# A two-layer diffusion backbone on one core: weight parts by casting and accumulating transfers, a three-step normalisation, attention outputs joined and laid out by DMA

## The chip, the cores and the metric

The kernel runs on one core of a Trainium2 chip. The metric is the device time of one execution in microseconds, read from the median of several runs. The core's engines are TensorE (PE; its weight loads are listed as PEld), VectorE (DVE), ScalarE (ACT), GpSimd (POOL) and SyncE (SP), which only issues transfers. SBUF is the memory on the core, PSUM the one into which TensorE writes, and DRAM the chip's own.

## The reference

The input is 512 latent tokens x and 256 context tokens of 1024 channels, and a conditioning vector. Two layers follow each other. The context tokens share the weights; in the second layer they are only needed for keys, values and scan states.

```
for l in range(DEPTH):                                    # 2
    z  = modulate(rms_norm(x, g1), shift, scale) @ w_in    # A: 1024, B: 2048, q, k, v, gates: 3*1024
    ya = rglru_bidir(z_A)      # short convolution, gates r and i by blocks of 64 channels,
                               # a = exp(-8 r softplus(-lam)), u = t i sqrt(1 - a^2), scan in both directions
    yb = spatial_gating(gelu(z_B))
    yc = windowed_attention(q, k, v, k_ctx, v_ctx, sink)   # 16 heads of 64, 4 key/value heads
    x  = x + ga1 * ((sigmoid(gate_a)*(ya@wa) + sigmoid(gate_b)*(yb@wb) + sigmoid(gate_c)*(yc@wc)) @ w_out)
    x  = x + ga2 * (relu(modulate(rms_norm(x, g2), ...) @ w1)**2 @ w2)
```

All of it is in 32-bit floating point.

## The kernel before, in words

**Products in three parts.** Each operand of a large product is split into a rounded part hi (type fp32r) and a remainder lo = src - hi, and the product is hi*hi + hi*lo + lo*hi, three matrix instructions. Activations are split by `split` (line 558): ScalarE copies into hi, VectorE subtracts. Weights come in blocks of 128x1024 (512 KB) through `weights` (line 562): SP's queue loads the tile wr, ScalarE rounds it into wh, and wl = wr - wh is computed by GpSimd where the flag `aside` is set, by VectorE elsewhere. There are three buffers each of wr, wh and wl, and 340 blocks in all.

**Stages of a layer.** First come keys, values and queries, and windowed attention (`attention`, line 1102): four groups of four heads, and in each group one unit for each 128 tokens (six units in layer 0, which carries the context too, four in layer 1). A unit is a softmax (`soft_part`) and the products with the values (`value_part`, line 1071). Between units stand pieces of the next group's queries and, from a list of 24 gate products (`gate_early`), some as filling: 16 in layer 0, 12 in layer 1. Then comes the recurrence (`lru`, line 1140), for eight blocks of 128 channels: a weight block and a block of gate weights (`lru_gates`, line 1131), convolution, gates, and a chain of elementwise instructions with two scans; the rest of the gate products stands between them. Then the merges of the three branches with the spatial gating between them, the output projection (`out_proj`, line 1350), a normalisation (`norm`, line 826), and the feed-forward (`ff`, line 1378). At the end of layer 0 `ff` runs the last part in two streams of tokens, normalises each for the next layer and computes its keys and values.

`aside` is set in the attention, in the part of the output projection that runs by streams, in the first part of the feed-forward, and in the step from layer 0 to layer 1.

**Attention outputs.** After the value products of a unit PSUM holds 128x512: the upper 64 partitions hold a correction that is added to the lower ones, with four heads side by side. Four copies on ScalarE and four additions on VectorE, each 64x128, place the four heads into two tiles of 128 channels. After the last unit of a group both tiles are stored to DRAM (`yd`) from ScalarE's queue; the merge of this branch reads them back through GpSimd's queue.

**Normalisation.** For each of eight channel tiles: VectorE multiplies x with the row factor, which stands in PSUM; ScalarE applies gain and shift; ScalarE copies into hi; VectorE subtracts for lo.

**Order.** All instructions are recorded with their tiles, and a planner (`Rec`, line 182 onward) orders them before they are emitted. Each has an assumed duration (`cost`) and a priority, by its place in the program and a boost for weight loads. The planner plays the engines forward: whichever engine is free takes the ready instruction of best priority, as long as buffers are free. Each engine then runs its instructions strictly in that order. The planner lengthens a VectorE instruction that reads two SBUF operands while GpSimd computes, and takes the size of a transfer from the tile.

Of the kernel before, what the change touches and what calls it, by code (L numbers as in the profile page):

```python
# [18 lines left out]
F32 = mybir.dt.float32  # L19
# [4 lines left out]
OP = mybir.AluOpType  # L24
# [157 lines left out]
class Rec:  # L182
# [91 lines left out]
    def commit(self, calls):  # L274
# [9 lines left out]
        if calls[0][2] == "dma_start":  # L284
            v = (calls[0][6] + calls[0][5])[0]
            op.nbytes = int(np.prod(v.base.shape)) * 4 if not v.base.part else 128 * 768 * 4
# [49 lines left out]
    def schedule(self):  # L336
# [90 lines left out]
        while events:  # L427
# [9 lines left out]
            for e in range(5):  # L437
                while free[e] <= now + 1e-6:
# [21 lines left out]
                    if op.both and free[POOL] > now and busy:  # L460
                        dur += min(0.7 * (free[POOL] - now), dur)
# [66 lines left out]
class Net:  # L528
    def __init__(self, rec, t):
        self.nc = self.rec = rec  # L530
        self.t = t
        self.n = 0
        self.wboost = BOOST
        self.aside = False
# [27 lines left out]
    def weights(self, l, blk):  # L562
        rec = self.rec
# [25 lines left out]
    def setup(self):  # L589
# [14 lines left out]
        self.one = self.ones[:, 0:1]  # L604
        self.neg = self.hold([128, 1], F32, name="neg")
        nc.vector.memset(self.neg, -1.0)
# [464 lines left out]
    def value_part(self, g, b, P, tiles, y2):  # L1071
# [23 lines left out]
        v4 = pv.rearrange("p (f j q) -> p f j q", f=2, j=2)  # L1095
        for f in range(2):
            nc.scalar.activation(y2[f][0:64, qs], v4[64:128, f, 0], AF.Copy)
            nc.vector.tensor_add(y2[f][0:64, qs], v4[0:64, f, 0], y2[f][0:64, qs])
            nc.scalar.activation(y2[f][64:128, qs], v4[0:64, f, 1], AF.Copy)
            nc.vector.tensor_add(y2[f][64:128, qs], v4[64:128, f, 1], y2[f][64:128, qs])  # L1100

    def attention(self, l, hs, W, ps):
# [9 lines left out]
        for g in range(4):  # L1112
            y2 = [self.slot([128, W]) for _ in range(2)]
            for u in range(nu):
                P, tiles = self.soft_part(g, u)
                self.finish(g, u, P, tiles, y2, nu)
# [8 lines left out]
    def finish(self, g, u, P, tiles, y2, nu):  # L1125
        self.value_part(g, u, P, tiles, y2)
        if u == nu - 1:
            for f in range(2):
                self.nc.scalar.dma_start(self.yd[2 * g + f], y2[f])

    def lru_gates(self, l, f):
        nc = self.nc
        gr = self.slot([128, 512])
        nc.sync.dma_start(gr, self.t["gate"][l, f])
        gh = self.slot([128, 512], F32R)
        gl = self.slot([128, 512], F32R)
        self.split(gr, gh, gl)
        return gh, gl

    def lru(self, l, hs, W):  # L1140
# [45 lines left out]
        def recur(pair):  # L1186
            for xc, out in pair:
                for d in range(2):
# [3 lines left out]
                    nc.scalar.activation(r, r, AF.Identity, bias=self.one)  # L1192
# [11 lines left out]
        def chain(xc, out, ss):  # L1204
            for d in range(2):
# [4 lines left out]
                nc.scalar.activation(r, t2, AF.Identity, scale=-0.5, bias=self.neg)  # L1210
# [139 lines left out]
    def out_proj(self, l, W):  # L1350
# [19 lines left out]
        for z in self.streams(W):  # L1370
            self.aside = True
# [6 lines left out]
    def ff(self, l, hs, W):  # L1378
# [33 lines left out]
        self.aside = True  # L1412
# [12 lines left out]
    def run(self):  # L1425
# [6 lines left out]
        for l in range(DEPTH):  # L1432
# [11 lines left out]
            self.aside = True  # L1444
            self.attention(l, hs, W, ps)
            self.aside = False
# [3 lines left out]
            self.aside = False  # L1450
# [124 lines left out]
```

## Time and profile before

| | us |
|---|---|
| median of 3 runs (lowest, highest) | 2715.12 (2712.99, 2715.19) |
| the profiled execution, time | 2712.24 |
| the profiled execution, span from first to last instruction | 2710.5 |
| PE busy | 2624.4 |
| DVE busy | 1868.3 |
| ACT busy | 1239.8 |
| POOL busy | 319.6 |

A busy time is the sum of the stretches in which the engine ran at least one instruction. All recorded instructions carry one line number (L507), that of the helper that emits them; so groups are told apart by tile names: s is any working tile in SBUF, p any in PSUM, t a small one, wr, wh and wl the weight tiles. An arrow s<-p,s reads: written <- read. "Idle before" is the time in which the engine had nothing to run just before the group's instructions, with the instruction that ended it. The chain of waits follows the work that ended last back from the end; PEclk is the clock that TensorE was granted, as a share of full speed.

### The profile page before, as it was taken

To read this page: it belongs to the slowest core of one execution; us is meant where nothing else is said; L and a number is where in the kernel's file an instruction comes from. 1 tells how busy PE (TensorE), PEld (TensorE's weight loads), DVE (VectorE), ACT (ScalarE), POOL (GpSimd) and SP (SyncE) were. 2 spreads that over 40 slices of the span, in tenths; PEclk is the share of its full clock that TensorE was granted. 3 is DMA by queue.
4 is the path that set the end of the run, shared out by engine and by line. 5 is a ranking of instruction groups with operands and counts; after the bars stand their busy time and mean duration, and the time that the engine had idled before them with its cause. 6 is when DMAs were issued, how large, how long until landed. Compare 5 with 4: busy or idle time off the path is not lost.

```text
span 2710.5 us, 38395 instructions
## 1 busy us (share of the span) xinstructions
PE 2624.4 (97%) x14916; PEld 2259.9 (83%) x14916; DVE 1868.3 (69%) x3528; ACT 1239.8 (46%) x2158; POOL 319.6 (12%) x229
## 2 busy tenths in 40 slices
PE   7999999989999999999999998999999999899999
PEld 4889988878898888888888877887888888888887
DVE  8887787996637758544444478999898666844444
ACT  4466668992122225222222254666996223532322
POOL 1111110111000034000000152120011001600000
PEclk9999999989999999999999989999999999999999
DMA  6112122456524423322222232122347555432322
GB/s 241 59 46 69 67 78 83 124 192 201 167 71 161 166 78 111 115 86 86 86 70 63 70 123 70 59 70 95 94 127 252 200 191 174 138 111 93 94 93 86
DMA packets 94391, 309.15 MB, mean 114 GB/s; under 512 B 11328, under 2 KB 11488, under 8 KB 94208
## 3 DMA queue, kind: packets, MB, share of 16 engines
q1 hardware_dynamic: 74592, 248.62, 28.6%
q0 software_dynamic: 10400, 37.09, 4.6%
q10 hardware_dynamic: 9216, 20.98, 2.0%
q8 instruction: 117, 1.92, 0.3%
q14 instruction: 66, 0.54, 0.1%
HBM read 270.99 MB, written 35.65 MB: 113 GB/s over the span
## 4 chain that ended last, share of the span: by engine, by line
PE 73%; DVE 12%; ACT 6%; DMA 4%; issue 4%; POOL 1%; POOLq 0%; SPq 0%; ACTq 0%; DVEq 0%
PE p L507 73%; DVE s L507 8%; ACT s L507 5%; DVE t L507 3%; DMA wr<-wmod 2%; DMA s<-wmod_k 1%; DVE junk L507 1%; POOL wl L507 1%; ACT wh L507 1%; DMA wr<-w 1%; ACT L507 1%; DVE wl L507 1%; DMA s<-x 0%; DMA gn<-qkg 0%; POOLq L1562 0%
## 5 line engine op out<-in xcount | busy, mean ns | idle before, releaser
L507 PE MATMUL p<-s,wh 128*128 128x512 f32 (+1 forms) x6816 | 1673.9, 353 | 6.3 <-DVE s L507 5.9
L507 PEld LDWEIGHTS p<-s,wh 128*128 128x128 f32 x6816 | 1194.7, 189 | 234.9 <-DVE s L507 7.8
L507 PE MATMUL p<-s,wl 128*128 128x512 f32 (+1 forms) x3408 | 1029.8, 352 | 0.3 <-POOL wl L507 0.3
L507 ACT ACTIVATE wh<-wr 128x1024 fp32r<-128x1024 f32 x340 | 360.4, 1061 | 929.6 <-PE p L507 648.1
L507 PEld LDWEIGHTS p<-s,wl 128*128 128x128 f32 x3408 | 572.2, 189 | 48.0 <-POOL wl L507 0.5
L507 DVE TENSOR_TENSOR wl<-wr,wh 128x1024 fp32r<-128x1024 f32 x240 | 294.7, 1228 | 288.3 <-ACT wh L507 285.8
L507 ACT ACTIVATE s<-p 64x128 f32<-64x128 f32 (+6 forms) x718 | 300.4, 452 | 209.8 <-PE p L507 196.1
L507 POOL TENSOR_TENSOR wl<-wr,wh 128x1024 fp32r<-128x1024 f32 x100 | 244.1, 2444 | 1202.7 <-ACT wh L507 1142.6
L507 DVE TENSOR_TENSOR s<-s,s 128x512 fp32r<-128x512 f32 (+5 forms) x409 | 333.8, 834 | 72.1 <-ACT s L507 68.6
L507 PE MATMUL p<-wh,s 128*128 128x256 f32 (+1 forms) x1472 | 303.7, 301 | 4.1 <-DVE s L507 3.5
L507 PE MATMUL p<-s,s 128*128 128x256 f32 (+3 forms) x1568 | 283.9, 322 | 22.5 <-ACT s L507 16.2
L507 ACT ACTIVATE s<-s 128x256 fp32r<-128x256 f32 (+6 forms) x349 | 203.5, 610 | 213.8 <-DVE s L507 201.2
L507 PEld LDWEIGHTS p<-s,s 128*128 128x128 f32 (+1 forms) x1568 | 222.1, 185 | 60.4 <-ACT s L507 21.1
L507 DVE SCALAR_TENSOR_TENSOR s<-p,mod,s 128x512 f32<-128x512 f32 (+1 forms) x222 | 138.1, 645 | 181.4 <-PE p L507 181.4
L507 PEld LDWEIGHTS p<-wh,s 128*128 128x128 f32 x1472 | 238.9, 191 | 16.8 <-DVE s L507 4.4
L507 DVE TENSOR_TENSOR s<-p,s 64x128 f32<-64x128 f32 (+4 forms) x444 | 201.9, 477 | 29.1 <-ACT s L507 23.1
L507 PE MATMUL p<-wl,s 128*128 128x256 f32 (+1 forms) x736 | 219.6, 298 | 0.4 <-DVE wl L507 0.4
L507 DVE SCALAR_TENSOR_TENSOR junk<-wr,condb 128x1024 bf16<-128x1024 f32 x128 | 156.4, 1222 | 73.1 <-DMA wr<-wmod 71.9
L507 PEld LDWEIGHTS p<-wl,s 128*128 128x128 f32 x736 | 140.2, 190 | 6.3 <-DVE wl L507 0.6
L507 ACT ACTIVATE s<-s,t,t 128x512 f32<-128x512 f32 (+1 forms) x128 | 109.8, 861 | 59.4 <-DVE t L507 59.2
L507 PE MATMUL p<-ident,s 128*128 128x128 f32 (+1 forms) x776 | 106.4, 279 | 23.8 <-DVE s L507 21.7
L507 DVE SCALAR_TENSOR_TENSOR s<-s,s 128x768 f32<-128x768 f32 x128 | 116.2, 950 | 12.5 <-ACT s L507 12.5
(87 smaller groups left out, 1322.7 us busy)
## 6 DMA issues: line engine op xcount, KB each, us to landing
wr<-w SPq DMA_DIRECT2D x340, 512.0 KB, 3.6
wr<-wmod SPq DMA_DIRECT2D x80, 512.0 KB, 4.0
gd<-s ACTq DMA_DIRECT2D x24, 384.0 KB, 2.9
s<-gd POOLq DMA_DIRECT2D x24, 384.0 KB, 5.8
s<-x SPq DMA_DIRECT2D x16, 384.0 KB, 6.4
gd<-s ACTq DMA_DIRECT2D x24, 256.0 KB, 2.1
s<-gd POOLq DMA_DIRECT2D x24, 256.0 KB, 5.6
s<-wmod_k SPq DMA_DIRECT2D x16, 256.0 KB, 6.4
```

The lines of the kernel that those rows point to most:

```text
L507: ins = getattr(getattr(self.nc, name), method)(*[r(x) for x in a], **{q: r(x) for q, x in k.items()})
```

## The change

1. In attention and recurrence the flag `cast` is set. `weights` then issues, from GpSimd's queue, a transfer that casts the block from DRAM into wh; ScalarE writes wl = -wh; and a second transfer from GpSimd's queue adds the block from DRAM onto wl. The recurrence's gate blocks are always read so. wr is not used there.
2. `aside` is never set any more, so all other blocks are subtracted on VectorE.
3. `norm`: VectorE multiplies x with gain and row factor in one instruction; ScalarE adds the shift and rounds into hi; VectorE computes (u + shift) - hi.
4. `value_part`: one copy of 64x512 on ScalarE and one addition on VectorE per unit; two stores per unit on SP's queue place the heads in DRAM. The function `finish` and the two group tiles go.
5. Recurrence: two instructions per direction move from ScalarE to VectorE, and the constant tile for them goes.
6. The planner takes the size of a transfer from its view, and lengthens a VectorE instruction by all of GpSimd's remaining time instead of at most 0.7 of it and at most once its own duration.

```diff
@@ commit
-            v = (calls[0][6] + calls[0][5])[0]
-            op.nbytes = int(np.prod(v.base.shape)) * 4 if not v.base.part else 128 * 768 * 4
+            v = [v for v in calls[0][6] + calls[0][5] if not v.base.part]
+            op.nbytes = 512 * v[0].width() if v else 128 * 768 * 4
@@ schedule
-                        dur += min(0.7 * (free[POOL] - now), dur)
+                        dur += free[POOL] - now
@@ weights
-        raw = self.wtile("wr", [128, 1024])
-        rec.sync.dma_start(raw, self.t["w"][l, blk])
+        raw = None if self.cast else self.wtile("wr", [128, 1024])
         hi = self.wtile("wh", [128, 1024], F32R)
         lo = self.wtile("wl", [128, 1024], F32R)
-        self.nc.scalar.activation(hi, raw, AF.Copy)
-        (self.nc.gpsimd if self.aside else self.nc.vector).tensor_sub(lo, raw, hi.bitcast(F32))
+        if self.cast:
+            rec.gpsimd.dma_start(hi, src)
+            rec.scalar.activation(lo, hi.bitcast(F32), AF.Copy, scale=-1.0)
+            rec.gpsimd.dma_start(lo, src, accum_op=OP.add)
+        else:
+            rec.sync.dma_start(raw, src)
+            rec.scalar.activation(hi, raw, AF.Copy)
+            (rec.gpsimd if self.aside else rec.vector).tensor_sub(lo, raw, hi.bitcast(F32))
@@ norm
-            nc.vector.tensor_mul(u, self.x[k][:, a:b], p)
-            nc.scalar.activation(u, u, AF.Identity, scale=G[:, i, k:k + 1], bias=self.mod[l][:, i, sh + k:sh + k + 1])
-            self.split(u, hs[k][0][:, a:b], hs[k][1][:, a:b])
+            shift = self.mod[l][:, i, sh + k:sh + k + 1]
+            h, lo = (t[:, a:b] for t in hs[k])
+            nc.vector.scalar_tensor_tensor(u, self.x[k][:, a:b], G[:, i, k:k + 1], p, op0=OP.mult, op1=OP.mult)
+            nc.scalar.activation(h, u, AF.Identity, bias=shift)
+            nc.vector.scalar_tensor_tensor(lo, u, shift, h.bitcast(F32), op0=OP.add, op1=OP.subtract)
@@ value_part
-        v4 = pv.rearrange("p (f j q) -> p f j q", f=2, j=2)
+        y = self.slot([128, 512])
+        nc.scalar.activation(y[0:64], pv[64:128], AF.Copy)
+        nc.vector.tensor_add(y[0:64], pv[0:64], y[0:64])
         for f in range(2):
-            nc.scalar.activation(y2[f][0:64, qs], v4[64:128, f, 0], AF.Copy)
-            nc.vector.tensor_add(y2[f][0:64, qs], v4[0:64, f, 0], y2[f][0:64, qs])
-            nc.scalar.activation(y2[f][64:128, qs], v4[0:64, f, 1], AF.Copy)
-            nc.vector.tensor_add(y2[f][64:128, qs], v4[64:128, f, 1], y2[f][64:128, qs])
+            d = self.yd[2 * g + f]
+            d = d._with(("rearrange", "(j d) q -> d j q", {"d": 64}), d.ix)
+            d = d._with(("get", (slice(None), slice(None), qs)), d.ix)
+            nc.sync.dma_start(d, y[0:64, f * 256:f * 256 + 256].rearrange("p (j q) -> p j q", j=2))
@@ finish, called after each unit
-        if u == nu - 1:
-            for f in range(2):
-                self.nc.scalar.dma_start(self.yd[2 * g + f], y2[f])
@@ lru_gates
-        nc.sync.dma_start(gr, self.t["gate"][l, f])
-        self.split(gr, gh, gl)
+        nc.gpsimd.dma_start(gh, src)
+        nc.scalar.activation(gl, gh.bitcast(F32), AF.Copy, scale=-1.0)
+        nc.gpsimd.dma_start(gl, src, accum_op=OP.add)
@@ recur and chain
-                    nc.scalar.activation(r, r, AF.Identity, bias=self.one)
+                    nc.vector.tensor_scalar(r, r, 1.0, None, op0=OP.add)
-                nc.scalar.activation(r, t2, AF.Identity, scale=-0.5, bias=self.neg)
+                nc.vector.tensor_scalar(r, t2, -0.5, -1.0, op0=OP.mult, op1=OP.add)
@@ out_proj, and ff before the step into layer 1
-            self.aside = True
@@ run
-            self.aside = True
+            self.aside, self.cast = False, True
             self.attention(l, hs, W, ps)
-            self.aside = False
             self.m = [None] * KT
             conds = (0,) if last else (0, 1)
             ya = self.lru(l, hs, W)
-            self.aside = False
+            self.cast = False
```

## Rows read from the trace of the kernel before

**Rows 1.** The page, part 1: busy us, share of span, instructions.

```profile
PE 2624.4 (97%) x14916; PEld 2259.9 (83%) x14916; DVE 1868.3 (69%) x3528; ACT 1239.8 (46%) x2158; POOL 319.6 (12%) x229
```

**Rows 2.** Stages: length, busy (instructions) of PE, PEld, DVE, ACT, POOL; PEclk, DMA, GB/s.

```profile
60.00:430.00 370.00, 360.72 (x2404) 323.02 (x2404) 301.08 (x835) 225.53 (x539) 55.30 (x23) 1.00 0.20 67
430.00:610.00 180.00, 167.39 (x941) 145.25 (x940) 161.46 (x223) 162.29 (x240) 14.04 (x22) 0.96 0.44 136
930.00:1056.00 126.00, 120.44 (x648) 102.91 (x647) 81.29 (x122) 44.13 (x62) 40.20 (x17) 0.97 0.30 95
1056.00:1540.00 484.00, 484.00 (x2786) 423.96 (x2785) 239.87 (x372) 123.67 (x204) 12.13 (x6) 1.00 0.27 85
1540.00:1660.00 120.00, 106.93 (x559) 91.96 (x558) 92.59 (x218) 55.00 (x95) 54.46 (x31) 0.91 0.33 107
1660.00:1862.00 202.00, 187.38 (x1205) 162.72 (x1204) 183.56 (x519) 132.12 (x307) 35.77 (x15) 0.98 0.19 63
1862.00:2010.00 148.00, 145.22 (x772) 122.78 (x772) 132.79 (x203) 135.18 (x207) 3.89 (x5) 0.99 0.32 97
2282.00:2372.00 90.00, 81.31 (x569) 76.56 (x569) 68.12 (x109) 47.19 (x85) 48.83 (x20) 0.94 0.40 128
```

**Rows 3.** Chain by line, of 430 to 610, 1660 to 1862, 2282 to 2372.

```profile
by line: PE p L507 46.9%; ACT s L507 31.0%; DVE s L507 7.5%; issue 5.7%; ACT L507 4.8%; ACT wh L507 3.9%; DVE t L507 0.3%; ACTq L507 0.2%
...
by line: PE p L507 38.2%; DVE s L507 36.8%; ACT s L507 10.1%; DVE t L507 9.1%; issue 5.5%; ACT t L507 0.3%; DVEq L507 0.1%; ACTq L507 0.1%
...
by line: issue 36.0%; POOL wl L507 25.0%; PE p L507 19.4%; DVE s L507 10.1%; DMA wr<-w 3.9%; POOLq L1562 2.7%; ACT s L507 2.0%; ACT wh L507 1.2%; POOLq L507 0.2%
```

**Rows 4.** Page, groups: busy us, mean ns | idle before them, and its releaser.

```profile
L507 ACT ACTIVATE wh<-wr 128x1024 fp32r<-128x1024 f32 x340 | 360.4, 1061 | 929.6 <-PE p L507 648.1
...
L507 DVE TENSOR_TENSOR wl<-wr,wh 128x1024 fp32r<-128x1024 f32 x240 | 294.7, 1228 | 288.3 <-ACT wh L507 285.8
...
L507 POOL TENSOR_TENSOR wl<-wr,wh 128x1024 fp32r<-128x1024 f32 x100 | 244.1, 2444 | 1202.7 <-ACT wh L507 1142.6
```

**Rows 5.** Groups of VectorE and ScalarE in 2282 to 2372, shapes kept apart.

```profile
L507 DVE TENSOR_TENSOR s<-s,s 128x256 f32<-128x256 f32 x14 | 18.9, 1352 | 3.9 <-ACT s L507 3.6
...
L507 DVE TENSOR_TENSOR s<-s,p 128x256 f32<-128x256 f32 x16 | 5.5, 414 | 0.3 <-PE p L507 0.3
...
L507 ACT ACTIVATE s<-s 128x256 fp32r<-128x256 f32 x21 | 7.8, 405 | 3.9 <-DVE s L507 3.9
```

**Rows 6.** Groups of VectorE in 1660 to 1862, shapes kept apart.

```profile
L507 DVE TENSOR_SCALAR s<-s,t 128x512 f32<-128x512 f32 x28 | 20.2, 781 | 0.2
...
L507 DVE TENSOR_TENSOR s<-p,s 64x128 f32<-64x128 f32 x52 | 14.9, 287 | 1.0 <-ACT s L507 0.4
...
L507 DVE TENSOR_TENSOR s<-p,s 64x512 fp32r<-64x512 f32 x6 | 4.1, 689 | 0.2
```

**Rows 7.** Groups of VectorE in 395 to 440, shapes kept apart.

```profile
L507 DVE TENSOR_SCALAR s<-s,t 128x640 f32<-128x640 f32 x8 | 4.0, 548 | 0.1
...
L507 DVE TENSOR_SCALAR s<-s,t 128x512 f32<-128x512 f32 x4 | 1.7, 480 | 0.0
```

**Rows 8.** Groups of ScalarE in 430 to 610, shapes kept apart.

```profile
L507 ACT ACTIVATE s<-s,ones 128x768 f32<-128x768 f32 x16 | 14.9, 959 | 0.0
...
L507 ACT ACTIVATE s<-s,neg 128x768 f32<-128x768 f32 x14 | 13.2, 946 | 2.9 <-DVE s L507 2.9
```

**Rows 9.** Transfers: size of each, median us from issue to landing.

```profile
wr<-w SPq DMA_DIRECT2D x340, 512.0 KB, 3.6
...
s<-yd POOLq DMA_DIRECT2D x8, 384.0 KB, 8.9
...
ya<-s POOLq DMA_DIRECT2D x8, 384.0 KB, 5.4
```

More of the change, by code (lines that the diff above doesn't have):

```diff
@@ L533, in __init__ @@
         self.wboost = BOOST
-        self.aside = False
+        self.aside = self.cast = False
     def slot(self, shape, dt=F32):
@@ L562, in weights @@
     def weights(self, l, blk):
-        rec = self.rec
+        rec, src = self.rec, self.t["w"][l, blk]
         rec.boost, was = self.wboost, rec.boost
-        raw = self.wtile("wr", [128, 1024])
-        rec.sync.dma_start(raw, self.t["w"][l, blk])
+        raw = None if self.cast else self.wtile("wr", [128, 1024])
         hi = self.wtile("wh", [128, 1024], F32R)
         lo = self.wtile("wl", [128, 1024], F32R)
-        self.nc.scalar.activation(hi, raw, AF.Copy)
-        (self.nc.gpsimd if self.aside else self.nc.vector).tensor_sub(lo, raw, hi.bitcast(F32))
+        if self.cast:
[6 more added lines that the diff above has]
+            (rec.gpsimd if self.aside else rec.vector).tensor_sub(lo, raw, hi.bitcast(F32))
         rec.boost = was
@@ L603, in setup @@
         nc.vector.memset(self.ones, 1.0)
-        self.one = self.ones[:, 0:1]
-        self.neg = self.hold([128, 1], F32, name="neg")
-        nc.vector.memset(self.neg, -1.0)
         self.junk = self.hold([128, D], BF16, name="junk")
@@ L1069, in soft_part, with value_part @@
         return P, tiles
-    def value_part(self, g, b, P, tiles, y2):
+    def value_part(self, g, b, P, tiles):
         nc = self.nc
@@ L1112, in attention @@
         for g in range(4):
-            y2 = [self.slot([128, W]) for _ in range(2)]
             for u in range(nu):
                 P, tiles = self.soft_part(g, u)
-                self.finish(g, u, P, tiles, y2, nu)
+                self.value_part(g, u, P, tiles)
                 if g < 3:
@@ L1123, in attention @@
                 self.fill((FILL_C if W > SEQ else FILL_X)[u])
-    def finish(self, g, u, P, tiles, y2, nu):
-        self.value_part(g, u, P, tiles, y2)
-        if u == nu - 1:
-            for f in range(2):
-                self.nc.scalar.dma_start(self.yd[2 * g + f], y2[f])
     def lru_gates(self, l, f):
         nc = self.nc
-        gr = self.slot([128, 512])
-        nc.sync.dma_start(gr, self.t["gate"][l, f])
+        src = self.t["gate"][l, f]
         gh = self.slot([128, 512], F32R)
         gl = self.slot([128, 512], F32R)
-        self.split(gr, gh, gl)
+        nc.gpsimd.dma_start(gh, src)
+        nc.scalar.activation(gl, gh.bitcast(F32), AF.Copy, scale=-1.0)
+        nc.gpsimd.dma_start(gl, src, accum_op=OP.add)
         return gh, gl
@@ L1443, in run @@
                          for f in range(KT)]
-            self.aside = True
+            self.aside, self.cast = False, True
             self.attention(l, hs, W, ps)
-            self.aside = False
             self.m = [None] * KT
@@ L1449, in run @@
             ya = self.lru(l, hs, W)
-            self.aside = False
+            self.cast = False
             self.later = [lambda f=f: self.mod_dve(l, f, conds) for f in range(16, 48)]
```

## The prediction, made before the change was run

> **What bounds the kernel now.** I read the page's busy line first, then a table of busy time by stage, then the chain of waits in the stages where TensorE has gaps, then the instruction groups of those stages, and the transfers last.
>
> TensorE is busy 2624.4 of 2710.5 us, VectorE 69%, ScalarE 46% [rows 1]. The matrix products are not touched by the change, so what it can win is TensorE's idle time, 86 us in all, and a little beside it: stalls too short to count as idle, and the slowing of the clock around gaps. The stage table says where the idle time lies: stage length less PE busy [rows 2]. The middle of layer 0 (1056 to 1540) has none, 484.00 of 484.00. The change bears on seven stages: key/value work and attention of layer 0 (60 to 430) 9.3 us, its recurrence (430 to 610) 12.6, its output projection and normalisation (930 to 1056) 5.6, the step into layer 1 (1540 to 1660) 13.1, attention of layer 1 (1660 to 1862) 14.6, its recurrence (1862 to 2010) 2.8, its output projection and normalisation (2282 to 2372) 8.7. Together 66.7 us: nearly the ceiling.
>
> Who makes TensorE wait there differs. In attention of layer 1 VectorE is busy 183.6 of 202 us and holds 45.9% of the chain (lines s and t); in the recurrence of layer 0 ScalarE is busy 162.3 of 180 us and its line s holds 31.0%; in 2282 to 2372 GpSimd's wl alone holds 25.0% [rows 2, 3].
>
> **GpSimd out of the subtraction.** Before, wl = wr - wh runs on GpSimd 100 times at 2.44 us: 24 + 20 blocks in the two attentions, 24 in the output projections, 16 in the first part of the feed-forward, 16 in the step into layer 1. On VectorE one takes 1.23 us [rows 4]. After it GpSimd subtracts no weights. While GpSimd subtracts, VectorE's instructions that read two operands from SBUF, and its fast single-operand ones, stand still: the 256-wide addition s<-s,s takes 1352 ns in 2282 to 2372, where GpSimd subtracts 20 times, and the same width with one operand in PSUM takes 414 in the same stage [rows 2, 5]; the 512-wide scaling takes 781 ns in attention of layer 1 and 480 where GpSimd is quiet [rows 6, 7].
>
> Attention of layer 1: that scaling alone gives 28 x (781 - 480) ns = 8.4 us; the whole of the GpSimd time, 15 subtractions or 35.8 us, is the upper end [rows 2, 6]. I take 16, nearer the lower end, since many of its instructions read PSUM. The joined outputs: 52 additions of 64x128 at 287 ns (14.9 us) become 13 of 64x512, which a row of that shape prices at 689 ns (9.0 us): 5.9 us less [rows 6]. VectorE thus loses 22 us; at its 45.9% of the chain this is 10 us for the end, inside the 14.6 us of idle. ScalarE's four copies of a unit become one as well; ScalarE has slack here (132 of 202 us).
>
> Key/value work and attention of layer 0 get the same, but only 9.3 us are idle: **4 us**.
>
> **Recurrence.** Two ScalarE instructions per direction and channel block (add 1; scale and subtract 1) go to VectorE. In 430 to 610 that takes 16 x 959 + 14 x 946 ns = 28.6 us off ScalarE [rows 8]. At 31.0% of the chain: 8.9, so **9 us**, under the 12.6 idle. VectorE gets 30 scalings of 768 columns; 548 ns for 640 and 480 for 512 [rows 7] extend to an estimate of 0.62 us each, 18.6 us. It loses about 14 weight subtractions, 17.2 us, and some gate splits: no net load. The second recurrence has 2.8 us idle: **1 us**.
>
> **Normalisation and the stages that lose GpSimd.** In 2282 to 2372 20 subtractions move to VectorE, 20 x 1.23 = 24.6 us more. The standstill that goes: 14 additions x (1352 - 414) = 13.1 us from one form alone, up to all of GpSimd's 48.8 us [rows 2, 5]. I call VectorE's load even. What falls is the delay of a block, 2.44 to 1.23 us, on a line with 25.0% of the chain: half of 22.5 us is more than the 8.7 idle. Behind it VectorE's own queue is late next, so I take 5 us, and 1 us for the step dropped from the normalisation (8 copies x 405 ns = 3.2 us of ScalarE per pass [rows 5], which partly lay under the projection): **6 us**. Bounds: VectorE now queues 24.6 us of subtractions before the additions that the normalisation waits for; if none of the standstill returned, at VectorE's 10.1% of the chain it would be 2.5 us worse; all idle recovered, 8.7 better. The step into layer 1 has 16 such subtractions and 13.1 us idle; its chain is mostly short dependent VectorE work that stays: **4 us**. Output projection of layer 0, 5.6 idle: **2 us**.
>
> **The cast and accumulating transfers.** In attention and recurrence 80 blocks (24 + 16 in layer 0, 20 + 20 in layer 1) and 16 gate blocks are no longer read on SP's queue and split by ScalarE and a subtraction. GpSimd issues a casting transfer into wh, ScalarE writes wl = -wh, and GpSimd issues a second transfer that adds the weights onto wl: 192 more issues on GpSimd's queue. Neither form stands in the trace: it has plain loads and an accumulation into DRAM. From below: a 512 KB load on SP lands in 3.6 us, so two and the 1061 ns pass of ScalarE make 8.3 us. From above: a load queued behind others on GpSimd's queue takes 8.9, twice and the pass 18.9 us. The nearest row is the accumulation from GpSimd's queue, 384 KB in 5.4 us: about 12 us for a block, which I take [rows 4, 9]. Before, with the weights loaded ahead into wr, it was 1.06 + 2.44 = 3.5 us from the moment wh and wl were free. Three buffers stand against it: attention of layer 0 needs a block per 370/24 = 15 us, of layer 1 per 202/20 = 10, the recurrence per 180/16 = 11. A buffer has three times that, 30 to 46 us, and a block's products use it for some 8 to 17. I cost the change at **nothing**: the cover is the other two blocks. If it is gone, each block costs what it comes late. Behind the second issue, which waits on GpSimd for ScalarE, stand the next block's first and the recurrence's accumulations into DRAM; behind ScalarE's negation, which waits for the first transfer, stand the evacuations of PSUM for which TensorE waits. That is the weak point.
>
> Here the Trainium skill speaks against the change: "SBUF — State Buffer", the box on the DVE that blocks DMA ("SBUF: two separate sides"), says that descriptors of a transfer issued by GpSimd can't be written while VectorE runs a two-port instruction, about 620 ns becoming 3100. The trace agrees only in part: loads from GpSimd's queue do land later than SP's, but its accumulations beside a VectorE that is busy 161 of 180 us have the 5.4 us above. By the page an issue would be 2.5 us later, a block about 5; the sum stands without it, and the second rival below has its own price.
>
> The 80 small output stores, two for each of 40 units, go on SP's queue instead of 16 on ScalarE's; SP then has no weights of these stages to carry, and the readers come only after the recurrence: nothing. The planner's two altered costs move the order; its rule on GpSimd's standstill meets almost no GpSimd arithmetic any more.
>
> **Sum.** 10 + 4 + 9 + 1 + 6 + 4 + 2 = 36 us. The profiled execution took 2712.24 us, 1.7 over its span; 2712.24 - 36 = 2676.2. The median of the three runs is 2.9 us above the profiled one: **2679 us**. Its own range is 2660 to 2698, from half the sum to half as much again.
>
> **Rivals.** First, the idle time moves: the order is planned anew and VectorE, still the fullest engine beside TensorE in the attentions and taking 30 scalings in each recurrence, sets new gaps. For it: VectorE is busy 132.8 of 148 us in the second recurrence. Against: its load there does not grow. A third of the sum is left: 2715 - 12 = 2703.
>
> Second, slower: ScalarE stands at the negation until a late casting transfer lands, and TensorE with it, in attention and recurrence. Price per block u, 80 blocks: the end is 36 us earlier and 80u later, and it decides from u = 0.45 us. At u = 0.8: 64 - 36 = 28, so 2743 us. For it: a cast from memory has no row, and GpSimd's loads reach 8.9 us in a burst. Against: three buffers, and blocks are needed 10 us apart, so bursts of these are rare.
>
> Third, more: all 66.7 us of idle time goes: 2712.2 - 66.7 + 2.9 = 2648, and short stalls within busy time might add some. Against: the kernel's own start and chains of short instructions stay.
>
> **Chances.** Forecast 0.55, first rival 0.18, second 0.15, third 0.12. A difference below 0.2%, 5.4 us, can't be told from none. The first rival ends within that in a quarter of its cases, the second in a tenth: faster 0.80, same 0.06, slower 0.14. The range 2640 to 2722 holds forecast, first and third rival, and leaves out most of the second and the far end of the third.
>
> **What would show it.** Right: no GpSimd wl; the 512-wide scaling in attention near 480 ns; PE busy in the second attention's stage with about 5 us of idle instead of 14.6; the 12 us gap at the end of the first recurrence mostly gone; the casting transfer landing in 4 to 6 us. Wrong: ScalarE or TensorE waiting for DMA on wh or wl for tens of us in total, first landings over 8 us, or the recurrences longer than 180 and 148 us.

## The result: slower by half a per cent, and the profile after

The changed kernel takes 2729.53 us (median of four runs, 2725.88 to 2733.33), the kernel before 2715.14 (2712.99 to 2715.19): ratio 1.0055, interval 1.0038 to 1.0072. Forecast was 2679, some 36 us faster than before, so the sign is wrong. The profiled execution took 2727.14 us, with a span of 2725.4.

The page's busy line of the changed kernel, against [rows 1]:

```profile
PE 2628.1 (96%) x14916; PEld 2259.2 (83%) x14916; DVE 1777.5 (65%) x3475; ACT 1156.0 (42%) x1929; POOL 217.2 (8%) x321
```

VectorE lost 91 us and ScalarE 84, and TensorE's idle time still grew, from 86.1 to 97.3 us. The waits of the kernel before (engine and tile <- what it waited for: us in total, times, longest) show who stops TensorE:

```profile
PE p L507 <- DVE s L507: 58.0, 40, 6.9
```

and those of the changed kernel:

```profile
ACT wl L507 <- DMA wh<-w: 119.7, 47, 6.6
...
PE p L507 <- DVE s L507: 32.7, 26, 6.2
...
PE p L507 <- DMA wl<-w: 31.7, 14, 7.9
```

The relief is there, 25.3 us less waiting for VectorE. In its place stand 31.7 us of waiting for the accumulating transfer, and ScalarE stands 119.7 us at its negation until a casting transfer lands. Of the 31.7 us, 22.1 fall in the two attentions and the step into layer 1. Attention 1 alone has 12.8 of them, which is all of TensorE's idle time there (200.00 - 187.15 us; waits of 1650 to 1850):

```profile
PE p L507 <- DMA wl<-w: 12.8, 8, 3.2
```

**Stage by stage.** Stages shift in time, so I compare them at the same amount of matrix work: each matrix instruction, in the order of its trace, counts with the usual interval from its issue to the next (0.232 us for 512 columns), and a stage ends in each trace where the sum is what it was at the bound of the kernel before. The table is worked out from the traces; its third column is an experiment told below (before, with GpSimd's subtractions on VectorE).

```
stage (us in before)              before  after  GpSimd out  predicted change
60-430     key/value, attention 0   370   371.6    358.3        -4
430-610    recurrence 0             180   182.2    179.0        -9
610-930    its end, merge           320   320.8    320.1         0
930-1056   projection, norm 0       126   117.6    117.0        -2
1540-1660  step into layer 1        120   116.4    107.9        -4
1660-1862  attention 1              202   199.3    193.2       -10
1862-2010  recurrence 1             148   162.0    148.2        -1
2010-2282  its end, merge           272   290.1    280.3         0
2282-2372  projection, norm 1        90    84.9     82.9        -6
```

The rows of the changed kernel for these stretches (columns as in [rows 2]; the merge of layer 1 added):

```profile
57.00:429.00 372.00, 360.02 (x2407) 322.66 (x2406) 263.02 (x756) 212.47 (x462) 41.64 (x59) 1.00 0.45 102
429.00:611.00 182.00, 170.42 (x940) 146.39 (x940) 153.82 (x225) 142.60 (x213) 39.26 (x55) 0.97 0.72 180
932.00:1049.00 117.00, 116.20 (x645) 99.85 (x645) 75.41 (x133) 39.28 (x53) 0.00 (x0) 1.00 0.33 99
1534.00:1650.00 116.00, 104.23 (x556) 88.41 (x554) 89.19 (x218) 46.38 (x78) 12.01 (x19) 0.94 0.41 114
1650.00:1850.00 200.00, 187.15 (x1212) 165.14 (x1211) 157.83 (x486) 126.69 (x264) 24.73 (x33) 0.97 0.46 103
1850.00:2012.00 162.00, 150.47 (x774) 125.22 (x773) 124.93 (x199) 123.63 (x183) 40.20 (x55) 0.97 0.74 166
2012.00:2302.00 290.00, 276.20 (x1398) 229.04 (x1397) 194.91 (x294) 104.45 (x142) 28.76 (x48) 0.98 0.67 207
2302.00:2387.00 85.00, 79.91 (x570) 75.46 (x569) 64.92 (x134) 41.22 (x70) 0.00 (x0) 0.96 0.50 144
```

The two stages of projection and normalisation together gain more than predicted, 13.5 us against 8. The attentions and the step into layer 1, the stages with most to win, give 5 us of the 18 predicted, though in attention 1 VectorE's load falls from 183.56 to 157.83 us, 25.7 us where the prediction had 22. The second recurrence and what follows lose 32.

The transfers (us from issue to landing) and the negation in the page of the changed kernel:

```profile
L507 ACT ACTIVATE wl<-wh 128x1024 fp32r<-128x1024 f32 x80 | 84.7, 1060 | 121.1 <-DMA wh<-w 119.7
...
wr<-w SPq DMA_DIRECT2D x260, 512.0 KB, 3.7
wh<-w POOLq DMA_DIRECT2D x80, 512.0 KB, 5.6
wl<-w POOLq DMA_DIRECT2D x80, 512.0 KB, 5.7
```

One block as it goes wrong, in the timeline of GpSimd, then of ScalarE and TensorE (start, us, what, idle before):

```profile
2044.98 0.54 POOL L507 DMA_DIRECT2D wh<-w  x1 [1.44 <-PE p L507]
2048.05 1.16 POOL L507 DMA_DIRECT2D s<-ya  x2 [2.54 <-DMA gd<-s]
...
2052.05 0.87 POOL L507 DMA_DIRECT2D wl<-w  x1 [0.94 <-ACT wl L507]
```

```profile
2050.69 1.06 ACT L507 ACTIVATE wl<-wh 128x1024 fp32r<-128x1024 f32 x1 [2.30 <-DMA wh<-w]
```

```profile
2050.80 0.64 PE L507 MATMUL p<-s,wh 128*128 128x512 f32 x2
2059.31 0.79 PE L507 MATMUL p<-s,wl 128*128 128x512 f32 x1 [7.87 <-DMA wl<-w]
```

The cast is issued when TensorE lets go of the buffer, ScalarE waits for it, the accumulation goes out and lands, and TensorE has stood 7.87 us: 2059.31 - 2044.98 = 14.3 us for the chain (cast, negation, accumulation) where I had 12. Over all 80 blocks the chain, worked out from the trace, takes 13.7 us in the median and 10.7 to 29.0; in the attentions the median is 13.3.

### The profile page after: what moved, and what is told of

Same layout as the page of the kernel before. It is cut to its first block, busy times and chain, and to the rows that moved or that the text cites. A ratio compares the mean times of both kernels' runs of the same rounds, so it can differ in the third digit from the quotient of the medians.

```text
span 2725.4 us, 38238 instructions
## 1 busy us (share of the span) xinstructions
PE 2628.1 (96%) x14916; PEld 2259.2 (83%) x14916; DVE 1777.5 (65%) x3475; ACT 1156.0 (42%) x1929; POOL 217.2 (8%) x321
## 4 chain that ended last, share of the span: by engine, by line
PE 57%; issue 22%; DMA 8%; DVE 7%; POOL 3%; ACT 3%; SPq 0%; POOLq 0%; ACTq 0%; DVEq 0%
PE p L507 57%; DVE s L507 5%; DMA wh<-w 3%; DMA wr<-w 2%; POOL wl L507 1%; DVE wl L507 1%; ACT s L507 1%; DMA ya<-s 1%; DMA wr<-wmod 1%; POOL wh L507 1%; DMA wl<-w 1%; ACT wh L507 1%; POOL s L507 1%; DVE t L507 0%; ACT wl L507 0%
## 5 line engine op out<-in xcount | busy, mean ns | idle before, releaser
L507 PE MATMUL p<-s,wl 128*128 128x512 f32 (+1 forms) x3408 | 1030.7, 352 | 21.2 <-DMA wl<-w 20.1
L507 ACT ACTIVATE wh<-wr 128x1024 fp32r<-128x1024 f32 x260 | 275.6, 1060 | 932.8 <-PE p L507 624.3
L507 DVE TENSOR_TENSOR wl<-wr,wh 128x1024 fp32r<-128x1024 f32 x260 | 317.9, 1223 | 319.7 <-ACT wh L507 316.8
L507 ACT ACTIVATE s<-p 128x512 f32<-128x512 f32 (+6 forms) x598 | 282.0, 509 | 225.6 <-PE p L507 216.1
L507 DVE TENSOR_TENSOR s<-s,s 128x768 fp32r<-128x768 f32 (+5 forms) x345 | 247.8, 731 | 51.1 <-ACT s L507 46.5
L507 ACT ACTIVATE s<-s 128x512 fp32r<-128x512 f32 (+6 forms) x301 | 183.2, 630 | 210.2 <-DVE s L507 184.2
L507 DVE TENSOR_TENSOR s<-p,s 128x512 fp32r<-128x512 f32 (+4 forms) x324 | 184.2, 596 | 87.2 <-ACT s L507 83.8
L507 PEld LDWEIGHTS p<-wl,s 128*128 128x128 f32 x736 | 141.0, 192 | 18.3 <-DMA wl<-w 12.9
L507 ACT ACTIVATE wl<-wh 128x1024 fp32r<-128x1024 f32 x80 | 84.7, 1060 | 121.1 <-DMA wh<-w 119.7
L507 PE MATMUL p<-ident,s 128*128 128x128 f32 (+1 forms) x776 | 107.3, 277 | 11.7 <-DVE s L507 10.1
```

What stands on the lines that cost most here:

```text
L507: ins = getattr(getattr(self.nc, name), method)(*[r(x) for x in a], **{q: r(x) for q, x in k.items()})
```

## Experiments

First the scatter, since nearly every edit makes the planner draw a new order. I made a change of the planner that has no meaning for any theory, 0.05 us more for the transfers that GpSimd doesn't issue, to the changed kernel and to the version with GpSimd's subtractions out:

```diff
-                        end = dma + 1900
+                        end = dma + 1900 + (0 if e == POOL else 50)
```

> The changed kernel with the planner told that transfers of the other queues (not GpSimd's) land 0.05 us later: a change of no meaning to any theory, which draws the order anew. If the order alone scatters times by 15 us or more, it falls outside 2714 to 2745, and the 34 us that the later landing for GpSimd's transfers gave back could be luck. If the planner's wrong landing time is the cause, it stays within 12 us of the changed kernel: 2718 to 2742.

> The kernel before with its weight subtractions on VectorE (2667) and the same change of no meaning in the planner. If its 46 us are the removal of GpSimd's arithmetic and not a lucky order: 2655 to 2682. If luck: 2690 or more.

Measured 2728.53 (1.0 lower) and 2675.88 (8.5 higher). Differences of 9 us between two orders prove nothing by themselves. Two new orders don't bound the scatter either, so I trust differences of some 20 us and more, and smaller ones only where several runs agree. The kernel before, run beside each experiment, had medians from 2712.1 to 2715.2, so differences between experiments carry some 3 us of their own. Intervals in brackets are those of the ratio to it.

**What costs: the cast.** The changed kernel without it (SP loads, ScalarE rounds, VectorE subtracts; the gate blocks too, whose own load and tile are not shown):

```diff
-            self.aside, self.cast = False, True
+            self.aside = self.cast = False
...
-        nc.gpsimd.dma_start(gh, src)
-        nc.scalar.activation(gl, gh.bitcast(F32), AF.Copy, scale=-1.0)
-        nc.gpsimd.dma_start(gl, src, accum_op=OP.add)
+        self.split(gr, gh, gl)
```

> The changed kernel with the casting transfers taken back: weight blocks of attention and recurrence come through wr on SP's queue, ScalarE rounds, VectorE subtracts; gate blocks are split as before. All other parts of the change stay. Late-part theory: TensorE's 32 us of waits for wl transfers and the longer second recurrence go, and the other parts show their worth: 2690 to 2702 us, below the kernel before. Rival, order and VectorE load: the loss lies in the new order and in the subtractions moved to VectorE, which now gets 80 more of them (98 us): 2725 us or more.

2695.01, ratio 0.993 (0.9917 to 0.9943), as the late-part theory had it. The cast costs 34.5 us in the changed kernel, 0.43 per block of 80. And the kernel before with the cast alone (the lines of the change put in, `self.aside, self.cast = False, True` ahead of the attention):

> The kernel before with the cast and accumulating transfers alone, for the weight blocks of attention and recurrence and the gate blocks; everything else as before, GpSimd's subtractions in projection and feed-forward too. Late-part theory: it is the slowest part, TensorE waits for wl by 30 us or more: 2730 to 2745 us. Rival: taking 44 GpSimd subtractions and 36 VectorE ones away helps, 2695 to 2710 us, and the loss of the changed kernel comes from its other parts.

2778.01, ratio 1.0241 (1.0228 to 1.0254): direction right, size missed by 33 us. Beside 38.6 us of TensorE's waits on wl, TensorE waits 26.4 us for ScalarE, which still carries the operations that the change moves.

**Landing time or buffers?** The planner assumes issue + 512 KB at 360 bytes/ns + 1.9 us, about 4 us for a transfer that takes 5.6. Four runs follow: the planner told 1.7 us more for every transfer of GpSimd's queue; four buffers of wh and wl instead (and two buffers fewer for the working tiles s); both; and the first with the cast alone on the kernel before:

```diff
-                        end = dma + 1900
+                        end = dma + 1900 + (1700 if e == POOL else 0)
...
-SLOTS = 48
-CAPS = {"slot": SLOTS, "ps": 8, "wr": 3, "wh": 3, "wl": 3}
+SLOTS = 46
+CAPS = {"slot": SLOTS, "ps": 8, "wr": 3, "wh": 4, "wl": 4}
```

> The changed kernel, but the planner assumes that a transfer issued by GpSimd lands 1.7 us later than it assumed (1.9 + 1.7 us after its data time, which for 512 KB gives the 5.6 us that the trace shows). No instruction is added or removed, only the order moves. If the loss is that the order was planned for earlier landings: 2700 to 2715 us, waits for wl under 10 us. If the loss is the time of the chain itself, which three buffers can't cover in the recurrence: within 6 us of the changed kernel's 2729.

> The changed kernel with four buffers of wh and of wl instead of three, and 46 working slots instead of 48. If too few buffers for the longer chain cost the time: 2700 to 2715 us, waits for wl under 10 us, because a block can start one block's use earlier. If ScalarE's waits for the first transfer or the order are the cause, buffers alone change little: 2722 to 2735 us. Two slots fewer may cost some us under either.

> The changed kernel with both cures: the planner assumes landings of GpSimd's transfers 1.7 us later, and there are four buffers of wh and wl with 46 working slots. If lateness is one cause that both cures treat: 2688 to 2698 us, no better than the later landings alone by more than 5 us. If buffers and plan are separate losses, the gains of 34 and 20 us add up to a good part: under 2685 us.

> The kernel before with the casting transfers alone, whose 66 us of loss are to be explained, and the planner told of landings 1.7 us later. If that loss too is an order planned for earlier landings: 2705 to 2730 us. If it is the chain itself, beside a ScalarE that is fuller here than in the changed kernel: 2755 us or more.

2695.57 (0.9926 to 0.9949), 2709.05 (0.9979 to 0.9996), 2685.57 (0.9887 to 0.9914), and 2737.57 (1.0075 to 1.0102) where the cast alone had 2778. The first came out 4 us below its range. The third, 10 us below the first, lies between the ranges of its two theories, and so does the fourth: these two totals decide nothing, and the stages have to. With 0.85 and 3.4 us in place of 1.7:

> The changed kernel with the planner told that GpSimd's transfers land 0.85 us later than it assumed, half of the 1.7 us that the trace of the changed kernel shows. If the wrong landing time is the cause, the time lies between 2729 and 2696: 2700 to 2722. If order luck: anywhere from 2690 to 2740, with no such order.

> The same with 3.4 us, twice what the trace shows. If the wrong landing time is the cause, nothing much is left to win beyond 1.7 us: 2685 to 2705. If later is simply always better (an earlier issue at any price): under 2685. If luck: over 2710.

2698.34, 2 us below its range, and 2694.96. The first 0.85 us bring 31 us, the rest nothing that counts, while the waits fall steadily. In turn for 0.85, 1.7 and 3.4 us:

```profile
ACT wl L507 <- DMA wh<-w: 57.7, 29, 6.0
...
PE p L507 <- DMA wl<-w: 19.1, 11, 6.9
```

```profile
ACT wl L507 <- DMA wh<-w: 37.2, 16, 5.8
...
PE p L507 <- DMA wl<-w: 11.7, 7, 2.7
```

```profile
ACT wl L507 <- DMA wh<-w: 12.0, 8, 4.1
...
PE p L507 <- DMA wl<-w: 7.4, 4, 3.3
```

That reads like one cause, and it is two. The stages summed in groups (worked out as above, us; "two operations moved" is an experiment told below). Each row comes from one profiled execution; that of the kernel without the cast took 2687.32 us, 7.7 under its median.

```
kernel                              attentions, step  recurrences, merges  norms
before                                    692.0             920.0          216.0
GpSimd out                                659.4             927.5          199.8
GpSimd out, two operations moved          658.8             954.3          198.9
after, no cast                            655.7             946.5          201.7
after                                     687.3             955.1          202.5
after, landing +0.85 / +1.7 / +3.4     685/693/688       928/918/924     202/202/202
after, four buffers                       662.8             958.7          201.3
after, +1.7 and four buffers              659.6             944.8          202.2
after, no second transfer                 661.3             941.6          201.5
```

In the attentions and the step the landing time that the planner believes changes nothing; a fourth buffer gives 24.5 us. In the recurrences and merges a fourth buffer changes nothing, and the longer landing time gives 37. The pair on the kernel before says the same: with the cast alone and then with 1.7 us more, the attentions and the step take 706.9 and 703.3 us, the recurrences and merges 970.9 and 934.6. The waits alone would mislead: with 1.7 us more, TensorE's waits on wl in the attentions and the step fall from 22.1 to 6.7 us, and these stages take as long as before. The 1.7 us also go to the gate blocks (6.5 us to landing) and to the recurrence's accumulations into DRAM; which transfers' lateness the 37 us belong to was not separated. Two runs ask about the attentions: a chain half as long with three buffers, which leaves the second transfer out, and four buffers without the cast.

```diff
-            rec.gpsimd.dma_start(lo, src, accum_op=OP.add)
```

> The changed kernel without the accumulating transfer of the weights: wl stays -wh, so the lo products are left wrong; a block's chain is the cast and ScalarE's negation, about 7 us instead of 14, with three buffers and the planner as changed. Theory: in the attentions and the step into layer 1 the cost of the cast (687 us of matrix stages against 656 without the cast) is the length of the chain against three buffers, so these stages fall to 655 to 668; the recurrences, where the planner's short landing costs, fall by half or more of 30 us; in total 2680 to 2705. Rival: these stages lose by the casting transfer itself or by its place on GpSimd's queue: they stay at 680 or more, and the total over 2712.

> The changed kernel without the cast, with four buffers for wh and wl. Control: if four buffers help only because the cast's chain is long, the attentions and the step stay at 651 to 661 us (656 with three) and the total within 2686 to 2704 (2695 with three). If four buffers are worth 20 us to any kernel, as they were to the changed one: 2680 or less.

2687.64 (0.9891 to 0.9918), with 661.3 us in these stages: the length of the chain against three buffers is the cost there (the recurrences fall by 13.5, a little less than half of the 30 that the expectation names). Leaving the second transfer out also takes 80 transfers off GpSimd's queue, and the cast lands in 4.5 us instead of 5.6; but the fourth buffer brings the same stages to 662.8 with both transfers in place. And 2707.80 (0.9974 to 0.9992), with 665.8 in these stages: 3.8 and 4.8 above my bounds and 12.8 slower than with three, so four buffers by themselves are no gift. Whether the fourth buffer or the two working buffers fewer cost that was not run apart.

The cast in the attentions alone (`self.cast = False` ahead of the recurrence, its gates by `split`):

> The changed kernel with the casting transfers in the attentions only; weight and gate blocks of the recurrences come through wr on SP's queue and are split by ScalarE and VectorE. Late-part theory, with the loss in the recurrence, where a comparison at equal finished matrix work shows +14 and +28 us against the kernel before: 2695 to 2706 us. If the attention's transfers cost as much: 2715 us or more.

2731.55 (1.0058 to 1.0083): missed by 26 us. By that expectation nearly all of the cost lay in the recurrences; the attentions' share is 33.9 us (689.6 against 655.7). Taking the cast out of the recurrences alone gives nothing back, 2731.55 against 2729.53: without it the ends of the recurrences have gaps of their own, which come after the next experiment.

**What gains: GpSimd out.** The kernel before with its flag off, VectorE doing all 340 subtractions:

```diff
-            self.aside = True
+            self.aside = False
```

> The kernel before with all 340 weight subtractions on VectorE, none on GpSimd; nothing else changed. If the standstill beside GpSimd cost as I reckoned (some 121 us of VectorE time over the run for 100 subtractions, which themselves are 123 us on VectorE), VectorE's load is even and the time is 2700 to 2715 us. If GpSimd's share was worth its standstill: 2718 us or more. If the removal of GpSimd carries the gain that the changed kernel without casting transfers shows: near 2697.

2667.34, ratio 0.9828 (0.9815 to 0.9842): 45.7 us under the kernel before that ran beside it, from one flag in three places, 30 us below the lowest of my expectations and faster than both kernels. Its busy line:

```profile
PE 2611.2 (98%) x14916; PEld 2250.4 (84%) x14916; DVE 1856.1 (70%) x3628; ACT 1237.4 (46%) x2156; POOL 75.6 (3%) x129
```

VectorE does 100 subtractions more and is busy 12 us less than before. TensorE's wait for it falls to

```profile
PE p L507 <- DVE s L507: 26.9, 26, 6.6
```

and of the 41.5 us that the span lost, 28.3 were TensorE idle and 13.2 lay inside what counts as busy.

**The two operations moved from ScalarE to VectorE**, put on that version, and taken out of three others:

```diff
-                    nc.scalar.activation(r, r, AF.Identity, bias=self.one)
+                    nc.vector.tensor_scalar(r, r, 1.0, None, op0=OP.add)
...
-                nc.scalar.activation(r, t2, AF.Identity, scale=-0.5, bias=self.neg)
+                nc.vector.tensor_scalar(r, t2, -0.5, -1.0, op0=OP.mult, op1=OP.add)
```

> The kernel before with its weight subtractions on VectorE (2667 us in the run with that alone) and now also the recurrence's two ScalarE operations (add 1; scale by -0.5 and subtract 1) moved to VectorE; no cast, no joined outputs, no three-step normalisation. Theory A, that the move sets a new gap at the end of each recurrence, where VectorE now works through the moved scalings ahead of the splits that TensorE waits for: 2683 to 2695 us, a stall of TensorE of more than 10 us at the end of a recurrence. Theory B, the prediction's step on the recurrence (9 us less in the first, 1 in the second), with VectorE relieved nothing else: 2655 to 2662. Rival C, no effect: 2664 to 2671, and the difference between the two versions without a cast (2695 and 2667) lies in the normalisation, the joined outputs or the planner's costs.

> The changed kernel without the casting transfers (weights and gates read on SP's queue, subtractions on VectorE) and without the two moves of the recurrence. What is left of the change: three-step normalisation, joined outputs, the planner's two costs. Theory A (the moves cost the version without a cast its 28 us): 2650 to 2668. Rival (the normalisation, the outputs or the planner's costs do): 2688 to 2700, as with the moves.

> The changed kernel with the planner told that GpSimd's transfers land 1.7 us later, four buffers for wh and wl, and the recurrence's two operations back on ScalarE. With the moves this was 2685.6. Theory A (the moves set gaps): 2665 to 2680. If the moves cost nothing here: 2682 to 2690. If they gained: over 2690.

> The changed kernel with only the recurrence's two operations back on ScalarE; cast, plan and three buffers as changed (2729.5 with the moves). If the moves cost what theory A says and the cost adds to the cast's: 2700 to 2712. If the cast's late blocks hide it: 2722 to 2735. If the moves give what the prediction said (10 us): 2737 to 2742.

2694.29 (0.9911 to 0.994), 2678.16 (0.9851 to 0.9881), 2705.01 (0.996 to 0.9984) and 2747.24 (1.0102 to 1.0144). So the move costs 27.0 and 16.9 us without the cast, and gains 19.4 and 17.7 with it: theory A has the first right, the direction of the second (10 us above its range), and is refuted for the two with the cast. The trace shows where. Against the version with GpSimd out, the move wins 11.4 us in the first recurrence, where the prediction had put 9, and loses 16.9 and 20.5 us in the ends and merges behind the two recurrences (the change of no meaning moved these two by -1.3 and 7.7). Behind the first recurrence TensorE has one long wait:

```profile
605.55 1.22 PE L507 MATMUL p<-s,wh 128*128 128x512 f32 x3 [13.71 <-DVE s L507]
```

The end of the second recurrence, same matrix work, in the version with GpSimd out:

```profile
1925.00:2060.00 135.00, 131.87 (x622) 108.17 (x621) 126.87 (x159) 113.19 (x155) 19.75 (x33) 1.00 0.58 179
```

with the move on top, and TensorE's one long wait in it:

```profile
1932.00:2086.00 154.00, 134.56 (x620) 110.63 (x620) 131.48 (x174) 88.07 (x119) 20.58 (x34) 0.93 0.51 155
```

```profile
2039.30 0.79 PE L507 MATMUL p<-s,wh 128*128 128x512 f32 x1 [17.31 <-DVE s L507]
```

and in the changed kernel:

```profile
1963.00:2115.00 152.00, 136.01 (x617) 110.42 (x616) 117.60 (x159) 86.09 (x116) 34.62 (x53) 0.96 0.79 213
```

VectorE had 126.87 of 135 us to do already; the moved scalings make it 131.48, its queue is full (16.79 busy of the 17 us from 2022 to 2039), and TensorE waits behind it for an operand that VectorE writes. With the cast VectorE has no weights to subtract there, 117.60. The stretch is as long, 152 us, but without the move it takes 158.3 (worked out as above), and TensorE waits there 11.7 us for wl, 4.9 for ScalarE and 1.0 for VectorE. Most of what the move gives with the cast lies in the first recurrence: 197.1 us without it and 182.2 with it, with TensorE's waits for ScalarE down from 16.0 to 5.4 us. That the room on VectorE is what turns the sign fits all four pairs; no run varied it by itself.

## Why the prediction was wrong, point by point

**The step that failed: "I cost the change at nothing: the cover is the other two blocks."** It costs 34.5 us with the recurrence's move and 69.1 without it. The prediction had the rival (the second) and its place right. Its u of 0.45 us per block was set against a gain of 36 us; the 0.43 measured would by itself have left the kernel even with before. It came out slower because the rest of the change gave 20.1 us (2715.1 to 2695.0) and not 36, of which more below.

The cover failed twice, by different causes. In the attentions and the step three buffers don't hide a chain of 13.3 us in the median: 31.6 us, whatever the plan. I had compared the mean need of a block, 10 to 15 us, with three times that. Even so the margin was thin: 12 us of chain and up to 17 of use, a range that no row backed, against 30 in attention 1. That TensorE lacks filling blocks while a softmax runs would explain why the mean misleads, but it was not tried; the trace has 12.8 us of direct waits on wl in attention 1, 5.6 in the step and 3.7 in attention 0, the rest behind other waits. In the recurrences the order spends the cover: the planner sets each issue for a landing of about 4 us, so real ones of 5.6 and 5.7 come late, with 37 us to be had there by 1.7 us in one line. Little of that shows in the price of the cast, 955.1 against 946.5 us, since without the cast TensorE has two long waits for VectorE in these stages, of 13.1 and 18.6 us.

For the landing itself my 5.4 us from the accumulation into DRAM [rows 9] was near, and the trace of the kernel before had a closer row that I passed over, plain loads of the same size on GpSimd's queue:

```profile
wr<-sgub POOLq DMA_DIRECT2D x2, 512.0 KB, 5.4
```

The Trainium skill, "DMA: Bandwidth & Descriptors", section "Anatomy of one DMA — SWDGE (gpsimd) path", fits 2.0 us plus bytes at 436 GB/s, 3.2 us by my estimate for 512 KB; the trace disagrees, with 5.6 and 5.7. The prediction's doubt about descriptors held up by VectorE does not show in the issues: the 80 of wh take 0.65 us and those of wl 0.91 in the mean, 1.4 and 1.7 at most. Whether it has a part in the landing, 3.8 to 10.8 us for the cast, the trace does not tell.

**GpSimd out: right in kind, mis-sized.** The terms that it shared with the joined outputs and the normalisation, 10 + 4 + 6 + 4 + 2 (attention 1, attention 0, norm 1, step, norm 0), sum to 26 us; alone, in the same stages, it gives 8.8 + 11.7 + 7.1 + 12.1 + 9.0 = 48.7. I had capped each stage by its idle time [rows 2], which is no ceiling: key/value and attention 0 had 9.3 us idle and gave 11.7, norm 0 had 5.6 and gave 9.0. What counts as busy shrank as well, from 360.72 and 120.44 us to

```profile
60.00:418.00 358.00, 355.99 (x2400) 321.49 (x2401) 303.70 (x855) 223.85 (x536) 0.00 (x0) 1.00 0.21 69
...
917.00:1034.00 117.00, 116.71 (x647) 100.28 (x647) 74.69 (x134) 44.54 (x61) 0.00 (x0) 1.00 0.32 101
```

In norm 0 the granted clock rose from 0.97 to 1.00; in the other it was 1.00 before too, and what shortened the busy time there is not shown. The sizes of VectorE's relief stood in my own rows: the 512-wide scaling fell to 481 ns where I had read 480, and the addition that took 1352 to 419, here in the changed kernel (attention 1, then norm 1):

```profile
L507 DVE TENSOR_SCALAR s<-s,t 128x512 f32<-128x512 f32 x28 | 11.7, 481 | 0.1
...
L507 DVE TENSOR_TENSOR s<-p,s 64x512 f32<-64x512 f32 x13 | 8.9, 681 | 5.0 <-ACT s L507 4.9
```

```profile
L507 DVE TENSOR_TENSOR s<-s,s 128x256 f32<-128x256 f32 x14 | 5.8, 419 | 0.2
```

The Trainium skill, "SBUF — State Buffer", section "Who interferes with whom", states that a VectorE instruction with two SBUF inputs contends with a GpSimd instruction that reads SBUF. The trace agrees, 1352 against 419 ns.

**Recurrence, -10.** Right on its own condition, "no net load": 17.7 us in the changed kernel, and 19.4 with the later landing and four buffers. It sank under the cast's late blocks. The term hung on the cast, which the sum did not say: with the cast out the same move costs 27.0 us, and my first rival, VectorE setting new gaps, is what happens. The moved scaling itself takes 549 ns for 768 columns where I had estimated 0.62 us.

**Joined outputs and three-step normalisation.** Together with the planner's two costs they make 2694.29 into 2695.01 (GpSimd out and the move, against the changed kernel without the cast): VectorE loses 13.6 us (1885.0 to 1871.4) and the time doesn't move, and without the move it is 10.8 us slower, close to the scatter. None of the three was run by itself. The 681 ns addition was priced at 689 [rows 6].

**The sum, step by step.** 2715.1 - 47.8 (GpSimd out) + 27.0 (move) + 0.7 (outputs, normalisation, planner's costs) + 34.5 (cast) = 2729.5. Taken in another order the same parts read -47.8, +10.8, +69.1 (cast without the move), -17.7: the move and the cast only make sense together.

What stays open: the best of both, four buffers in the attentions and three with the right landing time in the recurrences (about 660 and 918 us in the table), was not tried. With both settings everywhere the recurrences go back to 944.8, for which I have no shown reason; without the cast, too, four buffers and two working buffers fewer left these stages longer, 956.3 us against 946.5.

**The signs I named.** Right: no GpSimd wl, the scaling at 481 ns, the cast landing in 5.6 us, and the 12 us wait at the end of the first recurrence gone (TensorE's longest wait for ScalarE is 3.1 us). Wrong: attention 1 keeps 12.9 us of idle instead of 5, ScalarE waits 119.7 us for wh, and the recurrences take 182 and 162 us.

## What to carry to other kernels

Ask of a new kind of transfer not only whether buffers cover it, but what the order was planned with: here a landing time 1.7 us short in the planner cost 34 us of 2729. Price a removed contention by every instruction that it slowed, not by the idle time of its stage. Split a change of many parts by running its smallest part alone: here one flag was worth more than all the rest, and the rest gave it away.

## What the runs showed of the hardware

A 512 KB load that casts, or adds into SBUF, on GpSimd's queue lands in 5.6 and 5.7 us, against 3.7 for a plain one on SP's and 5.4 for the two plain ones on GpSimd's own. The cast's median differs between the runs: 4.5 us without the second transfer, 6.3 with four buffers. And a stall is paid for longer than it lasts. Here are windows of the changed kernel around the 7.87 us wait (last three columns: granted clock, DMA share, GB/s):

```profile
2040.00:2051.00 11.00, 11.00 (x49) 8.82 (x48) 10.92 (x15) 8.36 (x12) 3.72 (x7) 1.00 0.92 273
2051.00:2059.00 8.00, 0.44 (x2) 0.01 (x1) 6.61 (x10) 5.57 (x7) 2.41 (x4) 0.72 1.05 253
2059.00:2063.00 4.00, 3.69 (x9) 2.92 (x10) 4.00 (x6) 0.63 (x1) 0.00 (x0) 0.50 1.00 184
2063.00:2067.00 4.00, 4.00 (x15) 3.18 (x14) 1.96 (x3) 0.00 (x0) 1.36 (x3) 0.78 0.22 72
```

After TensorE stood still its clock was 0.50 of full speed, 1.2 of 2.4 GHz, for the next 4 us, and it did 9 instructions there where 4 us at full clock hold 18 (49 in 11 us).
